# Three families of 512-column matrix products written as two 256-column products each, with new places for their weights

## The chip, the cores and the metric

The kernel runs on one core of one Trainium2 chip. The metric is device time in microseconds of a whole execution, as the median of several runs. A core has a matrix engine (TensorE; the profile shows its products as PE and its weight loads as PEld), VectorE (DVE), ScalarE (ACT), GpSimd (POOL) and queues of DMA transfers, of which SyncE's (SP) carries most here. Each engine works through its own list of instructions in order and waits at semaphores for the others.

## The reference

The kernel computes a two-layer encoder for one sequence of 512 tokens and 1024 channels, in float32. Cut to what matters:

```python
for l in range(DEPTH):                                   # 2 layers
    h = rmsnorm(x, attn_norm[l])
    sb_q, sb_k, sb_v, df_q, df_k, df_v = split(h @ w_in[l], 6)     # 512 columns each
    sb_out = stick_breaking_attention(sb_q, sb_k, sb_v)  # 8 heads of 64, sigmoid weights
    df_out = differential_attention(rope(df_q), rope(df_k), df_v, lam)  # 4 heads, two softmaxes
    df_out = rmsnorm(df_out, subln_norm[l]) * (1.0 - lambda_init)
    x = x + concat([sb_out, df_out]) @ w_o[l]            # output projection
    h = rmsnorm(x, mlp_norm[l])
    x = x + square(relu(h @ w_ff1[l])) @ w_ff2[l]        # 4096 hidden channels
return rmsnorm(x, final_norm)
```

## The kernel before, in words

**Split products.** Every float32 weight tile is split into a rounded high part and the low remainder (`whi` by ScalarE at L118, `wlo` by VectorE at L135), and so are the activations (`h_hi`, `h_lo` and others). A product of two float32 tiles is then three matmuls: high by high, high by low, low by high. The helper `three` (L303 to L312) issues them; lines 310, 311 and 312 are these three for nearly all products of the kernel, so the profile's groups tell them apart by the tile that they write. Each matmul has a weight load of its own for its stationary operand of 128 x 128; the moving operand has 256 or 512 columns.

**Walking.** `three` has a last argument `step`. If it is set, the output in PSUM and the moving operand are addressed in blocks of `step` columns from the last block to the first (`walked`). The result is the same.

**Weight units.** `_UNITS` lists every 128 x 1024 weight tile in order of use. The first letter says what it is: `x` differential query and key blocks, `p` stick-breaking query and key blocks, `v` stick-breaking values, `w` the values of the differential (softmax) heads, `o` the output projection, `1` and `s` the first dense layer (its first group whole, the others in quadrants, seven forms each), `f` the second dense layer. `split_part` takes a slot of 1024 + 64 columns for each part and cuts 1024 columns out of it. For the letters in `NARROW`, `s` and `v`, the high part begins at column 48 and the low part at column 16 (`PLACES`); for all others both begin at 0. So what the diff calls places are offsets of the split weights inside their slots, in float32 columns of 4 bytes.

**Which operand is which.** In the projections (`block`), the output projection (`wo`) and the first stage of the dense layer (`quad_group`), the weights are stationary and activations move. In both kinds of values (`values_of`, `all_values`) the activations are stationary and the weights move.

**Widths.** `quad_group` and `values_of` multiply 256 columns at a time, walked with a step of 32. `block`, `all_values` and `wo` multiply 512 columns at a time, not walked.

**Order of the work.** Two generators are merged by hand. `dense` yields after each chunk of projections, values and the output projection's first half (`wo(1)`), with an assumed time; `attn` yields score, transpose and value products. After each step of `dense` a credit decides how many steps of `attn` follow. So in the first 214 us of layer 0 (and the same stretch of layer 1), products of attention stand between the chunks. The output projection's second half, `wo(0)`, comes after attention with nothing in between. The assumed times are constants (0.216 us for a wide product) that the change leaves alone. Instructions written in this order are placed on the engines by a list scheduler; `behind` adds an ordering edge where the text wants one. The product that `all_values` keeps as `W.product` is such an anchor, for the transposes of the first norm.

Of the kernel before, what the change touches and what calls it, by code (L numbers as in the profile page):

```python
# [22 lines left out]
KC = D // P  # L23
# [13 lines left out]
MAN = ()  # L37
APART = (("s", 0, 1), ("s", 3, 0), ("s", 3, 1))
_CTX = {}
NARROW, PLACES, PAD = "sv", (48, 16), 64  # L40
DLY_R, DLY_D, DLY_S, DLY_Q = 3.5, 10.2, 9.0, 6.0
TAIL, ATT, DENSE, CAP = 6.0, 53.0, 145.0, 0.1
FORMS = ("11", "x3", "x2", "21", "x1", "x4", "22")
# [9 lines left out]
def _unit_list():  # L53
    units = []
    def qk(l, cq, ck, b):
        units.append(("p", l, cq + b * P))
        units.append(("p", l, ck + b * P))

    for l in range(L):
        for item in ORDER:  # L60
            b = int(item[1])
            if item[0] == "d":
                units.append(("x", l, b, 0))
                units.append(("x", l, b, 1))
            elif item[0] == "s":
                qk(l, SBQ, SBK, b)
            elif item[0] == "w":
                units.extend(("w", l, part) for part in range(4))
            else:
                units.extend(("v", l, SBV + b * P, half) for half in range(2))  # L70
        for half in (1, 0):
            for j in range(4):
                units.append(("o", l, half, j))
        for g in range(GROUPS):
            if g == 0:
                units.extend(("1", l, f) for f in range(2 * GP))
            else:
                units.extend(("s", l, g, j, form) for j in range(2) for form in FORMS)
            for form in FORMS2:
                for c in range(GP // 2):  # L80
                    units.append(("f", l, g, form, c))
    return units


_UNITS = _unit_list()
# [9 lines left out]
class _Weights:  # L95
# [24 lines left out]
    def split_part(self, i, a, b):  # L120
        nc = self.nc
        if i not in self.tiles and i in self.home:
            self.tiles[i] = self.home[i]
        if i not in self.tiles:
            k = self.spot(i)
            self.owner[k] = i
            self.turn = k + 1
            hi, lo = (
                self.pools[k // 2].tile([P, 1024 + PAD], F32R, tag=f"w{n}", name=f"w{n}{i}")[:, at : at + 1024]
                for n, at in zip(("hi", "lo"), PLACES if _UNITS[i][0] in NARROW else (0, 0)))  # L130
            self.tiles[i] = (hi, lo)
        hi, lo = self.tiles[i]
        raw = self.first if (i, b) == (0, P) else self.raw[i]
        h = self.round(hi[:, a:b], raw[:, a:b])
        self.last = h, nc.vector.tensor_tensor(  # L135
            out=lo[:, a:b], in0=raw[:, a:b], in1=hi[:, a:b].bitcast(F32), op=ALU.subtract)
# [31 lines left out]
def trunk(ctx, tc, opened, xT, w, w2, w1, gfin, lamv, cos, sin, out):  # L168
# [11 lines left out]
    def bank(tag, name):  # L180
        if tag == "any":
            tag = ("mm", "s", "s", "mm", "s")[turn[0] % 5]
            turn[0] += 1
        ring[0] += tag == "s"
        return ps.tile([P, 512], F32, tag=tag, name=name, bufs=banks[tag])
# [3 lines left out]
    W = _Weights(nc, w, wraw, wspl)  # L189
# [37 lines left out]
    def gcol(which, l, c):  # L227
        i = {"attn": l * 8, "mlp": 16 + l * 8, "final": 32, "sub": 40 + l}[which] + c
        return g_all[:, i : i + 1]
# [21 lines left out]
    def make_h(c, g):  # L251
        a = nc.scalar.activation(h_hi[:, c, :], x[:, c, :], AF.Copy, scale=g)
        return a, nc.vector.scalar_tensor_tensor(
            out=h_lo[:, c, :], in0=x[:, c, :], scalar=g, in1=h_hi[:, c, :].bitcast(F32),
            op0=ALU.mult, op1=ALU.subtract)

    def add_sq(c, first, sqt, eng=nc.gpsimd):
        if first:
            return nc.scalar.activation(ssq, x[:, c, :], AF.Square), None
        sq = sqt("sq")  # L260
        s = nc.scalar.activation(sq, x[:, c, :], AF.Square)
        return s, eng.tensor_tensor(out=ssq, in0=ssq, in1=sq, op=ALU.add)
# [35 lines left out]
    def walked(t, step):  # L298
        return t.rearrange("p (a b) -> p a b", b=step)[:, ::-1, :]
# [4 lines left out]
    def three(pt, a, b, first, last, goes_on=False, step=0):  # L304
        ah, al = a
        bh, bl = b
        if step:
            pt, bh, bl = (walked(e, step) for e in (pt, bh, bl))
        return (
            nc.tensor.matmul(pt, ah, bh, start=first, stop=False, skip_group_check=goes_on),  # L310
            nc.tensor.matmul(pt, ah, bl, start=False, stop=False, skip_group_check=goes_on),  # L311
            nc.tensor.matmul(pt, al, bh, start=False, stop=last, skip_group_check=goes_on))  # L312

    def hpair(c):
        return h_hi[:, c, :], h_lo[:, c, :]

    def wpair(u, c, n=P):
        return u[0][:, c * n : (c + 1) * n], u[1][:, c * n : (c + 1) * n]

    def block(name, tag="mm"):  # L320
        pt = bank(tag, name)
        u = W.next("px" if name[0] == "p" else "1")
        for c in range(KC):
            three(pt, wpair(u, c), hpair(c), c == 0, c == KC - 1)
            yield pt if c == KC - 1 else None

    def constants(a2):
# [18 lines left out]
    for l in range(L):  # L346
        with ExitStack() as actx:
# [49 lines left out]
            first = W.split  # L397
# [56 lines left out]
            def all_values():  # L454
                pts = [bank(tag, f"p{l}w{tb}") for tb, tag in enumerate(("s", "s", "s", "o"))]
                for part in range(4):
                    u = W.next("w")
                    for n in range(2):
                        c = 2 * part + n
                        wide = wpair(u, n, 512)  # L460
                        for tb, pt in enumerate(pts):
                            h = [e[:, c, tb * P : (tb + 1) * P] for e in (h_hi, h_lo)]
                            W.product = three(pt, h, wide, c == 0, c == KC - 1)[2]
                            if c == KC - 1:
                                hi, lo, r = vd_hi[:, tb, :], vd_lo[:, tb, :], rcol[:, tb : tb + 1]
                                nc.scalar.activation(hi, pt, AF.Copy, scale=r)
                                nc.vector.scalar_tensor_tensor(
                                    out=lo, in0=pt, scalar=r, in1=hi.bitcast(F32), op0=ALU.mult, op1=ALU.subtract)
                            yield
                for i in range(4):  # L470
                    ready[("vd", i)] = clock[0] + 2.5
# [323 lines left out]
            def wo(half):  # L795
                for j in range(4):
                    u = W.next("o")
                    for dd in range(2):
                        db = 2 * j + dd
                        pt = bank("mm" if half else "any", f"wo{l}{half}{db}")  # L800
                        for e in range(4):
                            a = u[0][:, e * 256 + dd * P : e * 256 + dd * P + P]
                            b_ = u[1][:, e * 256 + dd * P : e * 256 + dd * P + P]
                            mh, ml = (md_hi, md_lo) if half else (ms_hi, ms_lo)
                            three(pt, (a, b_), (mh[:, e, :], ml[:, e, :]), e == 0, e == 3)
                            if e < 3:
                                yield 3 * 0.216
                        nc.vector.tensor_add(x[:, db, :], x[:, db, :], pt)
                        if half == 0:
                            ends["h"] = make_h(db, gcol("mlp", l, db))  # L810
                            add_sq(db, db == 0, tt, nc.vector)
                        yield 3 * 0.216

            def dense(pts):
# [24 lines left out]
                for item in ORDER[1:]:  # L839
                    kind, b = item[0], int(item[1])  # L840
                    for which in ("qk" if kind in "ds" else "v"):
# [12 lines left out]
                        if kind in "ds":  # L854
                            {"s": evict_s, "d": evict_d}[kind](pt, kind, b, which)
                yield from wo(1)

            at = attn()
            done = 2 * KC * 3 * 0.216 if l else 0.0
            spent = credit = 0.0  # L860
            live = True
            for cost in dense(pts if l else None):
# [5 lines left out]
                while live and credit > 0:  # L868
                    c = next(at, None)
# [14 lines left out]
            for _ in wo(0):  # L884
                pass

        with ExitStack() as fctx:
# [3 lines left out]
            last = l == L - 1  # L891
# [327 lines left out]
            for g in range(GROUPS):  # L1219
# [24 lines left out]
                for form in FORMS2:  # L1244
# [20 lines left out]
                    for n, (c, i, r, part) in enumerate(work):  # L1265
                        if c not in held:
                            held[c] = W.next("f")
                        u = held[c]
                        hi, lo = (e[:, :, i, :] for e in sides[c])
                        rs = slice(r * P, r * P + P)  # L1270
                        mine = [m for m, e in enumerate(work) if e[2:] == (r, part)]
                        pt, b_ = to[r], wpair(u, i, 512)
                        if part:
                            pt = halves[part - 1][:, 0:256]
                            b_ = [e[:, 256 * part - 256 : 256 * part] for e in b_]
# [8 lines left out]
                        if end and not last and form == "22" and n % 2:  # L1284
                            h = back(n // 2)
# [19 lines left out]
                    if end and last and form == "x1":  # L1305
                        done = ((2, 0), (3, 0), (0, 1), (1, 1))
                        squares = [square(*e) for e in done]
                        weighed = [weigh(*e) for e in done]
                    elif end and last and form == "x4":
                        first = [came[0]]  # L1310
# [5 lines left out]
            else:  # L1316
# [6 lines left out]
                for n in range(KC):  # L1323
                    if n in (3, 5):
                        for c_ in (n + 1, n + 2):
                            h = back(c_)
# [81 lines left out]
```

## Time and profile before

| | |
|---|---|
| runs | median 1107.52 us of 3 (1106.96, 1107.52, 1112.36) |
| profiled execution | 1108.1 us, its span 1106.3 us |
| granted TensorE clock | 0.999 of full speed |
| TensorE products | 6345, busy 1098.0 us |
| TensorE weight loads | 6345, busy 959.4 us |
| VectorE, ScalarE, GpSimd | busy 906.8, 688.1, 151.9 us |

The span is from the first to the last instruction of the program. A product's row in the timeline has its start and its modelled duration; since products are pipelined, the duration is longer than the distance to the next start. In a name such as `wo<-mdh,whi` the output comes first, then the two operands. `p0s1q` is layer 0's stick-breaking query block 1, `p0u` layer 0's stick-breaking values, `p0w` its softmax values, `wo` the output projection, `X`, `V` and `Y` the banks of the dense layers.

### The profile page before, as it was taken

Reading aid. Unit: us, or ns where it says so; the run is one execution under the profiler, and the core shown is the slowest. Engines: PE = TensorE matmul, PEld = TensorE weight load, DVE = VectorE, ACT = ScalarE, POOL = GpSimd, SP = SyncE. Lnnn points to the kernel's source line nnn. Section 1 sums busy time; section 2 is a strip of 40 time slices with the busy share of each in tenths; the row PEclk is TensorE's granted clock in tenths of the full one; section 3 lists DMA queues with packets and bytes.
Section 4 is the critical chain, followed back from the end, with each engine's and each line's share of the span. In section 5 each row is a group of like instructions: output and inputs, shape, how many; then the busy total and the mean of one; then the engine's idle time right before and its main releaser. Section 6 shows DMA issues by size and latency. Waiting matters only on the chain.

```text
span 1106.3 us, 17170 instructions
## 1 busy us (share of the span) xinstructions
PE 1098.0 (99%) x6345; PEld 959.4 (87%) x6345; DVE 906.8 (82%) x1333; ACT 688.1 (62%) x1131; POOL 151.9 (14%) x233
## 2 busy tenths in 40 slices
PE   9999999999999999999999999999999999999997
PEld 7889889888899899899778898888888998998986
DVE  7799688798669879779877897887797798797797
ACT  6447777567658458467345576675674584574775
POOL 1001343101011001001000013530010110010010
PEclk9999999999999999999999999999999999999999
DMA  7466343269777788758325654522577787787462
GB/s 248 144 191 190 113 127 107 84 213 230 183 212 186 182 209 185 196 138 212 113 76 142 190 164 123 164 77 77 197 176 180 211 183 186 202 188 196 130 133 96
DMA packets 61044, 181.25 MB, mean 164 GB/s; under 512 B 7456, under 2 KB 8736, under 8 KB 60960
## 3 DMA queue, kind: packets, MB, share of 16 engines
q1 hardware_dynamic: 50160, 141.84, 41.1%
q0 software_dynamic: 10368, 37.75, 19.7%
q8 instruction: 50, 0.82, 0.3%
q10 hardware_dynamic: 432, 0.56, 0.1%
q14 instruction: 34, 0.28, 0.1%
HBM read 150.77 MB, written 4.19 MB: 140 GB/s over the span
## 4 chain that ended last, share of the span: by engine, by line
PE 93%; issue 3%; DVE 2%; DMA 2%; ACT 0%; POOL 0%; POOLq 0%; DVEq 0%; ACTq 0%
PE X L310 8%; PE X L311 8%; PE X L312 8%; PE V L311 3%; PE V L312 3%; PE V L310 3%; PE wo L310 3%; PE wo L311 3%; PE wo L312 3%; PE f L312 3%; PE f L310 3%; PE f L311 3%; PE Y L312 2%; PE Y L311 2%; PE Y L310 2%
## 5 line engine op out<-in xcount | busy, mean ns | idle before, releaser
L118 ACT ACTIVATE whi<-q 128x1024 fp32r<-128x1024 f32 x96 | 101.3, 1056 | 101.7 <-PE X L312 39.3
L135 DVE TENSOR_TENSOR wlo<-q,whi 128x1024 fp32r<-128x1024 f32 x96 | 116.8, 1221 | 43.0 <-ACT whi L118 42.8
L135 DVE TENSOR_TENSOR wlo<-raw,whi 128x1024 fp32r<-128x1024 f32 (+1 forms) x82 | 96.7, 1185 | 6.7 <-ACT whi L118 6.4
L118 ACT ACTIVATE whi<-raw 128x1024 fp32r<-128x1024 f32 (+1 forms) x82 | 80.8, 994 | 33.6 <-issue 17.9
L310 PE MATMUL X<-whi,Ah 128*128 128x512 f32 x248 | 97.6, 393 | 0.0
L312 PE MATMUL X<-whi,Al 128*128 128x512 f32 x248 | 96.7, 390 | 0.0
L311 PE MATMUL X<-wlo,Ah 128*128 128x512 f32 x248 | 96.6, 390 | 0.0
L135 DVE TENSOR_TENSOR wlo<-waves,whi 128x1024 fp32r<-128x1024 f32 x40 | 48.8, 1221 | 15.4 <-ACT whi L118 15.3
L118 ACT ACTIVATE whi<-waves 128x1024 fp32r<-128x1024 f32 x40 | 42.2, 1056 | 29.2 <-PE X L312 18.9
L310 PEld LDWEIGHTS X<-whi,Ah 128*128 128x128 f32 x248 | 46.5, 188 | 12.1 <-DVE y L1132 1.9
L312 PEld LDWEIGHTS X<-whi,Al 128*128 128x128 f32 x248 | 46.6, 188 | 9.9
L311 PEld LDWEIGHTS X<-wlo,Ah 128*128 128x128 f32 x248 | 46.6, 188 | 8.9
L311 PE MATMUL X<-h_lo,whi 128*128 128x256 f32 x192 | 53.0, 276 | 0.0
L310 PE MATMUL X<-h_hi,whi 128*128 128x256 f32 x192 | 53.0, 276 | 0.0
L312 PE MATMUL X<-hxh,wlo 128*128 128x256 f32 x192 | 53.0, 276 | 0.0
L310 PE MATMUL X<-hxh,whi 128*128 128x256 f32 x192 | 53.0, 276 | 0.0
L312 PE MATMUL X<-h_hi,wlo 128*128 128x256 f32 x192 | 53.0, 276 | 0.0
L311 PE MATMUL X<-hxl,whi 128*128 128x256 f32 x192 | 53.0, 276 | 0.0
L310 PE MATMUL f<-h_hi,whi 128*128 128x512 f32 x128 | 50.4, 394 | 0.0
L312 PE MATMUL f<-h_hi,wlo 128*128 128x512 f32 x128 | 49.9, 390 | 0.0
L311 PE MATMUL f<-h_lo,whi 128*128 128x512 f32 x128 | 49.8, 389 | 0.0
L242 DVE TENSOR_TENSOR Al<-x,Ah 128x512 fp32r<-128x512 f32 (+1 forms) x60 | 46.5, 792 | 3.7 <-ACT Ah L241 3.5
(764 smaller groups left out, 3686.7 us busy)
## 6 DMA issues: line engine op xcount, KB each, us to landing
raw<-in_w SPq DMA_DIRECT2D x78, 512.0 KB, 3.6
q<-in_w SPq DMA_DIRECT2D x48, 512.0 KB, 4.5
q<-in_w POOLq DMA_DIRECT2D x48, 512.0 KB, 8.5
waves<-in_w SPq DMA_DIRECT2D x28, 512.0 KB, 4.6
first_a<-in_w SPq DMA_DIRECT2D x12, 512.0 KB, 4.8
first_b<-in_w SPq DMA_DIRECT2D x12, 512.0 KB, 5.4
first_c<-in_w SPq DMA_DIRECT2D x12, 512.0 KB, 4.4
first_b<-in_w POOLq DMA_DIRECT2D x12, 512.0 KB, 6.7
```

Source lines behind the costliest of these rows:

```text
L118: return self.nc.scalar.activation(o, src, AF.Copy)
L135: self.last = h, nc.vector.tensor_tensor(out=lo[:, a:b], in0=raw[:, a:b], in1=hi[:, a:b].bitcast(F32), op=ALU.subtract)
L242: nc.vector.tensor_tensor(out=lo, in0=src, in1=hi.bitcast(F32), op=ALU.subtract)
L310: nc.tensor.matmul(pt, ah, bh, start=first, stop=False, skip_group_check=goes_on),
L311: nc.tensor.matmul(pt, ah, bl, start=False, stop=False, skip_group_check=goes_on),
L312: nc.tensor.matmul(pt, al, bh, start=False, stop=last, skip_group_check=goes_on))
```

## The change

`PLACES` becomes a table by letter. `p` and `o` get the pair (48, 16) that `s` has; `w` gets (16, 48); `v` goes from (48, 16) to (16, 48). A new helper `three_halves` issues the three products for the columns 0 to 255 and then for 256 to 511, each walked with a step of 32; only the very first opens the bank and only the very last closes it. The stick-breaking query and key blocks, the softmax values and the output projection call it in place of `three`. The differential blocks (`x`) and the dense layers keep what they had.

```diff
-NARROW, PLACES, PAD = "sv", (48, 16), 64
+PLACES, PAD = {"s": (48, 16), "p": (48, 16), "o": (48, 16), "v": (16, 48), "w": (16, 48)}, 64
...
-                for n, at in zip(("hi", "lo"), PLACES if _UNITS[i][0] in NARROW else (0, 0)))
+                for n, at in zip(("hi", "lo"), PLACES.get(_UNITS[i][0], (0, 0))))
...
+    def three_halves(pt, a, b, first, last):
+        for n in range(2):
+            cols = slice(256 * n, 256 * n + 256)
+            done = three(pt[:, cols], a, [e[:, cols] for e in b], first and n == 0, last and n == 1, True, 32)
+        return done
...
+        some = three_halves if _UNITS[W.used][0] == "p" else three
         u = W.next("px" if name[0] == "p" else "1")
         for c in range(KC):
-            three(pt, wpair(u, c), hpair(c), c == 0, c == KC - 1)
+            some(pt, wpair(u, c), hpair(c), c == 0, c == KC - 1)
...
-                            W.product = three(pt, h, wide, c == 0, c == KC - 1)[2]
+                            W.product = three_halves(pt, h, wide, c == 0, c == KC - 1)[2]
...
-                            three(pt, (a, b_), (mh[:, e, :], ml[:, e, :]), e == 0, e == 3)
+                            three_halves(pt, (a, b_), (mh[:, e, :], ml[:, e, :]), e == 0, e == 3)
```

## The prediction

> **What bounds the kernel now.** I read the page's head, its busy times and its chain of waits first, then the groups of TensorE instructions by line and shape, then the starts in the timeline of the stages that the change touches.
>
> ```profile
> span 1106.3 us, 17170 instructions
> PE 1098.0 (99%) x6345; PEld 959.4 (87%) x6345; DVE 906.8 (82%) x1333; ACT 688.1 (62%) x1131; POOL 151.9 (14%) x233
> PE 93%; issue 3%; DVE 2%; DMA 2%; ACT 0%; POOL 0%; POOLq 0%; DVEq 0%; ACTq 0%
> ```
>
> TensorE streams matmuls through the whole span, and 93% of the chain that ended last is its own. So the price of this change is the distance between the starts of successive products (I call it the pitch), times their number. Busy microseconds and mean durations overlap, because one product starts before the last one's modelled end; the pitch has to be read from starts.
>
> The pitch of a 512-column product where nothing is mixed in, from the output projection's second half in layer 0:
>
> ```profile
> 214.75 0.39 PE L310 MATMUL wo<-vdh,whi 128*128 128x512 f32 x1
> ...
> 236.51 0.39 PE L310 MATMUL f<-h_hi,whi 128*128 128x512 f32 x1
> L310 PE MATMUL wo<-vdh,whi x32: 389/389/389, 214.7 to 235.8; 128*128 128x512 f32 x32
> ```
>
> Three lines of 32 products each lie between those starts: (236.51 - 214.75) / 96 = 226.7 ns, and each lasts 389 ns. The pitch of a 256-column product in the walked form and at the first stage's places, which is the form the change copies:
>
> ```profile
> 318.79 0.28 PE L310 MATMUL X<-h_hi,whi 128*128 128x256 f32 x1
> 318.90 0.28 PE L311 MATMUL X<-h_lo,whi 128*128 128x256 f32 x1
> 319.02 0.28 PE L312 MATMUL X<-h_hi,wlo 128*128 128x256 f32 x1
> 319.14 0.28 PE L310 MATMUL X<-h_hi,whi 128*128 128x256 f32 x1
> ...
> 356.88 0.39 PE L310 MATMUL X<-whi,Ah 128*128 128x512 f32 x1
> ```
>
> Two quad groups of 168 products lie between 318.79 and 356.88 (7 forms, 2 pairs, 4 chunks, 3 products each): 38.09 / 336 = 113.4 ns. Two of them make 226.7 ns, the same as one wide product to 0.1 ns. The first two after the switch from wide products are slower (0.11 and 0.12), and from the third start on the pitch is constant: this form falls into step in two products.
>
> Two other rows show that 113.4 ns belongs to this form and these places and is not what 256 columns cost anywhere:
>
> ```profile
> 97.17 0.28 PE L312 MATMUL p0u<-whi,h_lo 128*128 128x256 f32 x1
> ...
> 99.05 0.28 PE L562 MATMUL S0d<-st0d3k,st0d3q 128*128 128x256 f32 x1
> 1097.50 0.28 PE L312 MATMUL Z<-whi,Al 128*128 128x256 f32 x1
> ...
> 1098.70 0.28 PE L310 MATMUL half<-whi,Ah 128*128 128x256 f32 x1
> ```
>
> The stick-breaking values (walked too, but with the weights as moving operand at 48 and 16) take 1.88 us for 16 starts, 117.5 ns. The last, unwalked 256-column pieces take 1.20 us for 10 starts, 120 ns.
>
> **The change, part by part.** Three families of 512-column products become pairs of halves: the stick-breaking query and key blocks (16 blocks of 8 chunks of 3 = 384), the softmax values (2 layers, 4 parts, 2 chunks, 4 banks, 3 = 192) and the output projection (2 layers, 2 halves, 8 columns, 4 chunks, 3 = 384). That is 960 matmuls and 960 weight loads more. The values of the stick-breaking heads (384 halves) keep their number and swap their pair of places.
>
> *What hides nothing and what costs nothing.* No DMA, wait, PSUM bank or eviction is added; a bank is still released by the last product of its group, which starts 113 ns later and lasts 276 ns instead of 389, so it ends when it did. The splits write at other offsets; their time does not depend on it:
>
> ```profile
> L118 ACT ACTIVATE whi<-raw x82: 295/1060/1107, 4.9 to 812.8; 128x1024 fp32r<-128x1024 f32 x74, 128x256 fp32r<-128x256 f32 x7, 128x128 fp32r<-128x128 f32 x1
> L118 ACT ACTIVATE whi<-first_a x24: 1060/1062/1064, 310.8 to 1040.0; 128x1024 fp32r<-128x1024 f32 x24
> ```
>
> The raw ones go to place 0 (all but the few value units), the first-stage ones to place 48, with medians of 1060 and 1062 ns. The added weight loads are one a half already in the rows at 113.4, so their cost is inside that figure.
>
> *Quiet stretches.* Half of the output projection (192 products) runs undisturbed at 226.7, and so do nearly all the softmax values, whose rows stand at the same 389 to 390 ns:
>
> ```profile
> L311 PE MATMUL p0w<-wlo,h_hi 128*128 128x512 f32 x16 | 6.2, 390 | 0.0
> L310 PE MATMUL p0w<-mdh,h_hi 128*128 128x512 f32 x16 | 5.9, 389 | 0.0
> ```
>
>  Projections and output projection have weights stationary and 256 contiguous activation columns moving, as the first stage has, and all these tiles are allocated on multiples of 256 bytes, so the distance between the address loaded and the address streamed is the first stage's. The values have the roles reversed, and the pair (16, 48) reversed with them, which makes the same distances, modulo 256 bytes, for high and low parts (64 bytes one way for the high, the other way for the low). So I price these halves at 113.4: 384 products x (2 x 113.4 - 226.7) = 0.0 us.
>
> *Stretches mixed with attention.* There the wide products are above their floor:
>
> ```profile
> L310 PE MATMUL p0s1q<-h_hi,whi 128*128 128x512 f32 x8 | 3.2, 404 | 0.0
> L312 PE MATMUL p0s1q<-h_hi,wlo 128*128 128x512 f32 x8 | 3.2, 394 | 0.0
> L311 PE MATMUL p0s1q<-h_lo,whi 128*128 128x512 f32 x8 | 3.2, 394 | 0.0
> L310 PE MATMUL wo<-mdh,whi 128*128 128x512 f32 x64 | 26.4, 412 | 0.0
> L312 PE MATMUL wo<-mdh,wlo 128*128 128x512 f32 x64 | 25.2, 394 | 0.0
> L311 PE MATMUL wo<-mdl,whi 128*128 128x512 f32 x64 | 25.2, 394 | 0.0
> L310 PE MATMUL p0u<-whi,h_hi 128*128 128x256 f32 x64 | 18.3, 286 | 0.0
> ```
>
> A mean above 389 ns (276 for halves) is pitch lost. For one projection block: 8 x (15 + 5 + 5) = 0.2 us, 3.2 us over 16 blocks; for the first half of the output projection: 64 x (23 + 5 + 5) = 2.1 us. A part of it is no loss: a product behind a row of transposes starts late only because the last transpose took too little.
>
> ```profile
> 137.34 0.93 PE L661 MATMUL T0s<-edge,sig0s 128*128 128x128 f32 x7
> 138.10 0.60 PE L273 MATMUL rs_d<-edge,sqo 128*128 128x128 f32 x4
> 138.46 0.48 PE L310 MATMUL p0s2k<-h_hi,whi 128*128 128x512 f32 x1
> 138.78 0.39 PE L311 MATMUL p0s2k<-h_lo,whi 128*128 128x512 f32 x1
> ```
>
> Eleven transposes end their starts in 1.12 us, and the next product then holds 0.32 us. Taking that 0.09 us off the 20 projections and 14 output products that stand so leaves about 1.5 us of true loss in the projections and 1.0 in the output projection. In the stick-breaking values it is 384 x (117.5 - 113.4) = 1.6 us.
>
> The halves would lose their first two pitches after every attention step, as at 318.79: together some 11 ns more than 226.7. The projections stand in 84 unbroken runs, the output projection in 55 mixed ones, and the stick-breaking values in 50, counted over the starts from the first to the last of these rows:
>
> ```profile
> 77.93 0.39 PE L310 MATMUL p0s0q<-h_hi,whi 128*128 128x512 f32 x1
> ...
> 710.71 0.39 PE L312 MATMUL p1s3k<-h_hi,wlo 128*128 128x512 f32 x1
> ```
>
> So: projections -1.5 + 84 x 0.011 = -0.6 us; output projection -1.0 + 55 x 0.011 = -0.4; stick-breaking values, whose new pair gives them the first stage's distance, -1.6 + 50 x 0.011 = -1.0. **Sum -2.0 us.** The unknown is the pitch of new halves in mixed stretches, bounded below by 113.4 with no falling into step to pay (-4.1 us in all) and above by the 117.5 of the stick-breaking values as they are now. I take the value near the lower end, because the cause that separates 113.4 from 117.5 in these rows, as far as the code shows, is the distance of addresses, and the change sets it to the first stage's everywhere.
>
> The profiled execution took 1108.1 us, 1.8 outside its 1106.3 us span, and the median of the runs is 1107.5. With 2.0 off: a span near 1104.3, a profiled execution near 1106.1 and a median of **1105.5 us**.
>
> **Rivals.**
>
> *Halves do not fall into step between attention steps.* Then they stand near the 117.5 ns of the stick-breaking values, which never settle although they come in runs of 6 to 18. For it: those values are the largest family of halves that the trace shows in this company. Against it: they have the other distance. Price, against the true mean of wide ones (389 + 3.9 and 389 + 5.2 ns in duration, so 230.6 and 231.9 in pitch): 384 x (235 - 230.6) + 192 x (235 - 231.9) = +2.3 us, and the swapped values gain nothing. It decides from 115.5 ns a half on. Time: 1109.8. If the quiet 384 products stayed out of step as well, 384 x 8.3 ns = 3.2 us more: 1113.0.
>
> *All halves are at the floor at once.* The whole 4.1 us go, and what the neighbouring score and value products lose to phase goes with it, bounded by another microsecond from their small number. For it: no engine other than TensorE is near its limit. Against it: the first two halves at 318.79. Time: 1102.4.
>
> *Every product pays a fixed price, whatever its form.* The nearest rows are the unwalked pieces at 120 ns: a pair of them takes 240, 13.3 ns more than a wide product, and 960 such pairs cost 12.8 us; the mixed stretches give back at most their 2.5. Time: 1117.8. For it: those pieces come from the same kind of product as the wide ones beside them. Against it: the 336 walked halves at 113.4, whose pair shows a price of 0.1 ns. The Trainium skill, page "TensorE: Matmul & The Clock Gate", section "Back-to-back issue gap", states such a price: a warm pitch of N / 2.4 + 2.5 ns, by which a pair costs 2.5 ns more than one product of 512, an estimate of 2.4 us over the 960 (1109.9). The trace does not agree with it: the formula gives 215.8 and 109.2 ns where the rows show 226.7 and 113.4.
>
> *The order of other engines moves.* The program's instructions are placed by a list scheduler that estimates durations; more, shorter products could change what VectorE and ScalarE do first. The longest wait of TensorE for a split shows what one such shift can cost:
>
> ```profile
> PEld V L311 <- DVE wlo L135: 1.2, 1, 1.2
> ```
>
> With TensorE at 99% busy such waits are rare; I give this case 1.2 us either way, 1108.7 at the upper end without the gain.
>
> **How the numbers follow.** The forecast 0.58; halves out of step 0.20 (a quarter of it in the quiet stretches as well); all at the floor 0.10; a fixed price 0.04; order 0.08. The range goes from the floor case to the first form of the slower one, with 0.4 us below and 1.2 above for pitches that were read from few rows: 1102.0 to 1111.0. It leaves out the two dear cases, 0.09. A difference of 0.5%, 5.5 us, is about what a measurement can tell from no change; the bounds are 1102.0 and 1113.1. Faster than that takes the floor case and something more, 0.06; slower takes halves out of step everywhere or the fixed price, 0.06; within, 0.88.
>
> **What would show each step right or wrong.** Matmuls should number 7305. Right: the output projection's second half still runs from 214.75 to about 236.5 in length (21.8 us), now in 192 starts at 113.4; the rows of the stick-breaking values drop from means of 280 to 286 ns to about 277; the halves of projections have means near 278. Wrong: means of 280 and more in the projections (out of step), a pitch of 115 or more in the quiet output projection (a fixed price or another distance), or new waits of TensorE on ScalarE's or VectorE's splits. What would make the prediction wrong as a whole is a pitch that follows something other than those distances: then the swapped values would not move, and the new halves could stand anywhere between 113 and 120 ns.

## The result, and the profile after

The changed kernel takes 1113.13 us (median of 6 runs, 1112.8 to 1113.53) against 1107.41 us for the kernel before beside it (median of 6, 1106.96 to 1112.36): a ratio of 1.005, with a 95% interval of 1.0039 to 1.0060. It is 5.7 us slower. The forecast was 1105.5 us in a range of 1102.0 to 1111.0, so the direction was wrong and the time lies outside the range. The profiled execution of the kernel before was one of its slower ones (1108.1 us, 0.7 above this median), so differences between the two traces come out somewhat smaller than 5.7 us.

The head of the changed kernel's profile, its busy times and its chain of waits by engine:

```profile
span 1111.4 us, 19077 instructions
PE 1102.3 (99%) x7305; PEld 1004.2 (90%) x7305; DVE 906.9 (82%) x1333; ACT 687.6 (62%) x1131; POOL 153.8 (14%) x233
PE 88%; DVE 5%; ACT 2%; DMA 2%; POOL 2%; issue 1%; SPq 0%; DVEq 0%; POOLq 0%; ACTq 0%
```

There are 7305 products, as announced, and the other engines do the same work in nearly the same time. The span grew by 5.1 us. In the chain TensorE's share fell from 93% to 88%, and VectorE's rose from 2% to 5%: the chain now passes through VectorE more often. That is the first sign of new waits.

The groups of the new halves (last columns: busy us, mean ns of one, idle us just before). A half that starts 113.4 ns after the last one reads 276 ns:

```profile
L310 PE MATMUL p0w<-whi,h_hi 128*128 128x256 f32 x32 | 9.0, 282 | 0.0
L311 PE MATMUL p0w<-wlo,h_hi 128*128 128x256 f32 x32 | 9.0, 282 | 0.0
L311 PE MATMUL p0w<-mdl,h_hi 128*128 128x256 f32 x32 | 8.9, 283 | 0.0
L310 PE MATMUL p0u<-whi,h_hi 128*128 128x256 f32 x64 | 18.4, 287 | 0.0
L310 PE MATMUL wo<-vdh,whi 128*128 128x256 f32 x128 | 35.3, 276 | 0.0
L311 PE MATMUL wo<-mdl,whi 128*128 128x256 f32 x128 | 35.8, 279 | 0.0
L310 PE MATMUL p0s1q<-h_hi,whi 128*128 128x256 f32 x16 | 4.5, 283 | 0.0
L311 PE MATMUL p0s1q<-h_lo,whi 128*128 128x256 f32 x16 | 4.5, 278 | 0.0
```

Only the output projection's quiet half (`vdh`) is at 276. The softmax values (`p0w`) stand at 282, though nothing is mixed into them, and the stick-breaking values (`p0u`) stand where they stood (287, before 286). The timeline gives the pitches:

```profile
29.98 0.28 PE L310 MATMUL p0w<-whi,h_hi 128*128 128x256 f32 x1
...
33.16 0.28 PE L310 MATMUL p0w<-whi,h_hi 128*128 128x256 f32 x1
...
218.35 0.28 PE L310 MATMUL wo<-vdh,whi 128*128 128x256 f32 x1
...
240.12 0.39 PE L310 MATMUL f<-h_hi,whi 128*128 128x512 f32 x1
...
1104.58 0.28 PE L312 MATMUL half<-whi,Al 128*128 128x256 f32 x1
```

Between the first two rows lie 27 halves of the softmax values: 3.18 / 27 = 117.8 ns. Between the next two lie the 192 halves of the quiet output projection: 21.77 / 192 = 113.4 ns, as forecast. The last row is the last product; before it started at 1100.02, so 4.56 us of the loss lie ahead of it, and the other 0.5 us of span behind it.

The rows of waits (engine, tile and line, what it waited for: us in total, times, longest) that the changed kernel has and the kernel before has not, or has smaller:

```profile
PEld rb_d L295 <- POOL rc L282: 0.8, 2, 0.4
PEld T0s L668 <- DVE turned L242: 0.4, 1, 0.4
PEld T1s L668 <- DVE turned L242: 0.4, 1, 0.4
PEld p1w L311 <- DVE mdl L135: 0.4, 1, 0.4
PEld O0s L699 <- DVE mt L715: 0.3, 1, 0.3
```

The 1.2 us wait of `V` for `wlo` that the prediction showed is gone. One of the new waits reads like this in the timeline:

```profile
155.50 0.68 DVE L715 TENSOR_TENSOR mt<-O0s,oc 64x512 f32<-64x512 f32 x1 [0.46 <-ACT hl0s2q L241]
...
155.89 0.28 PE L312 MATMUL p0s3q<-h_hi,wlo 128*128 128x256 f32 x1
156.24 0.39 PE L699 MATMUL O0s<-turned,vs 128*128 128x256 f32 x1
```

The value product at 156.24 waits for `mt`, and `mt` started only after ScalarE had written `hl0s2q`, work for other heads. TensorE's starts stand 0.35 us apart instead of 0.11.

**Where the 4.56 us came from.** For every product I took the distance to the next start and subtracted its floor (226.7 ns for 512 columns, half of that for 256, 109 for a transpose). What is left over is called a wait above 45 ns, and phase below. One execution of each kernel, in us:

| part | before | after | difference |
|---|---|---|---|
| softmax values, phase | 0.2 | 1.9 | +1.8 |
| stick-breaking values, phase | 1.65 | 1.8 | +0.2 |
| output projection, phase | 1.0 | 1.3 | +0.3 |
| stick-breaking projections, phase | 1.55 | 1.75 | +0.2 |
| everything else, phase | 4.05 | 3.4 | -0.65 |
| waits of attention's products and of the projections beside them | 0.7 | 3.8 | +3.1 |
| wait of `V` for `wlo` | 1.1 | 0.0 | -1.1 |
| other waits (opening, softmax values, dense layers) | 4.4 | 5.2 | +0.8 |

Most of the +0.8 of other waits is the opening's and says nothing of the change. The first softmax value starts at 16.99 us here and at 16.51 before, but it starts just as late, at 16.98, in a kernel that differs from the one before in two places of weights alone, and in no instruction's order (the fourth experiment). Where the -0.65 of phase in everything else comes from was not followed.

So there are two causes: halves that do not reach the pitch they were given (+1.8 in the softmax values, and +1.8 of phase in all), and waits that were not there (+3.1 around attention and the projections, less the 1.1 at `V` that went away). The lag can be followed at the same product in both traces: first stick-breaking projection +1.7, last one of layer 0 +3.6, unchanged through layer 0's dense layer (+3.6), +2.5 at the last norm's transposes of that layer (the wait of `V` is no longer needed, as TensorE arrives later than its data), end of layer 1's softmax values +3.4, last projection of layer 1 +4.4, last product +4.6. The dense layers, where nothing was changed, neither add nor give back, but for that one wait.

### The profile page after: what moved, and what is told of

Read it like the earlier page. It is cut to its first block, busy times and chain, and to the rows that moved or that the text cites. A ratio compares the mean times of both kernels' runs of the same rounds, so it can differ in the third digit from the quotient of the medians.

```text
span 1111.4 us, 19077 instructions
## 1 busy us (share of the span) xinstructions
PE 1102.3 (99%) x7305; PEld 1004.2 (90%) x7305; DVE 906.9 (82%) x1333; ACT 687.6 (62%) x1131; POOL 153.8 (14%) x233
## 4 chain that ended last, share of the span: by engine, by line
PE 88%; DVE 5%; ACT 2%; DMA 2%; POOL 2%; issue 1%; SPq 0%; DVEq 0%; POOLq 0%; ACTq 0%
PE X L310 9%; PE X L312 9%; PE X L311 9%; PE V L310 3%; PE V L311 3%; PE V L312 3%; PE wo L312 3%; PE wo L310 3%; PE wo L311 3%; PE f L312 3%; PE f L310 3%; PE f L311 3%; PE Y L312 2%; PE Y L311 2%; PE Y L310 2%
```

## Experiments

### One part at a time

Four kernels make one part of the change each; everything else is as before.

Only the softmax values as halves:

```diff
+PLACES, PAD = {"s": (48, 16), "v": (48, 16), "w": (16, 48)}, 64
...
-                            W.product = three(pt, h, wide, c == 0, c == KC - 1)[2]
+                            W.product = three_halves(pt, h, wide, c == 0, c == KC - 1)[2]
```

> Only the softmax values are halved, at their new places; projections, output projection and stick-breaking values are as before. Theory A (halves whose weights move never settle): means of 280 to 282 ns in the value rows instead of 276, about +1.8 us of pitch, so 1.5 to 2.5 us slower than before. Theory B (the loss is waits behind a new order of the other engines' instructions): only 9 instructions of VectorE and 1 of ScalarE stand elsewhere here, so nothing beyond the pitch. Theory C (each added product costs the same, 5.7 us / 960 = 5.9 ns): 192 x 5.9 ns = +1.1 us.

Measured: 1109.52 us beside 1107.38, ratio 1.0017 (1.0007 to 1.0026), 0.8 to 2.9 us slower. Their group in the profile of this kernel:

```profile
L311 PE MATMUL p0w<-wlo,h_hi 128*128 128x256 f32 x32 | 9.0, 282 | 0.0
```

The mean is that of the full change. The step "softmax values 0.0" is wrong by itself, without the rest.

Only the stick-breaking projections as halves:

```diff
+PLACES, PAD = {"s": (48, 16), "v": (48, 16), "p": (48, 16)}, 64
...
+        some = three_halves if _UNITS[W.used][0] == "p" else three
```

> Only the stick-breaking projections are halved, at their new places. Theory A: pitch within 0.3 us of before. Theory B: 44 instructions of VectorE and 12 of ScalarE stand elsewhere, so the new waits of score, value and transpose products (about 2 us in the changed kernel) are here: +1.5 to +2.5 us. Theory C: 384 x 5.9 ns = +2.3 us spread evenly over the projections' own rows, without waits.

Measured: 1111.11 beside 1107.38, ratio 1.0030 (1.0021 to 1.0040), 2.3 to 4.4 us slower. This is the largest part. The rows of waits of this kernel:

```profile
PEld rb_d L295 <- POOL rc L282: 0.7, 2, 0.4
PEld T0s L668 <- DVE turned L242: 0.4, 1, 0.4
PEld T1s L668 <- DVE turned L242: 0.4, 1, 0.4
```

Three of the five new waits of the full change are here already (the one for `turned` in layer 0 was 0.2 in the kernel before).

Only the output projection as halves, and only the swap of the stick-breaking values' places:

```diff
+PLACES, PAD = {"s": (48, 16), "v": (48, 16), "o": (48, 16)}, 64
...
-                            three(pt, (a, b_), (mh[:, e, :], ml[:, e, :]), e == 0, e == 3)
+                            three_halves(pt, (a, b_), (mh[:, e, :], ml[:, e, :]), e == 0, e == 3)
```

> Only the output projection is halved, at its new places. Theory A: its quiet half unchanged, its half mixed with attention +0.3 us. Theory B: 12 instructions of VectorE and 8 of ScalarE stand elsewhere, so little more: 0 to +0.7 us. Theory C: 384 x 5.9 ns = +2.3 us.

```diff
+PLACES, PAD = {"s": (48, 16), "v": (16, 48)}, 64
```

> Only the places of the stick-breaking values are swapped; the order of all engines is that of before. Theory A: the swap moves nothing, means stay at 279 to 286 ns, time within 0.3 us of before. The theory of the prediction (the distance of addresses sets the pitch): means of 277 ns, 1.0 us faster. Theory C: no product is added, no difference.

Measured: 1107.94 beside 1107.38, ratio 1.0005 (0.9996 to 1.0014), and 1107.98, ratio 1.0003 (0.9994 to 1.0013). Neither can be told from no change. The swap did not move its group by more than 1 ns:

```profile
L310 PE MATMUL p0u<-whi,h_hi 128*128 128x256 f32 x64 | 18.4, 287 | 0.0
L311 PE MATMUL p0u<-wlo,h_hi 128*128 128x256 f32 x64 | 18.0, 281 | 0.0
```

The -1.0 us forecast for it is not there. The four ratios add up to 1.0055 against 1.0050 for the whole; within the intervals, the parts act side by side.

### Is it the order of the other engines?

In the compiled programs the same instructions stand at another place in their engine's list: with only the projections changed, 12 of ScalarE, 44 of VectorE and 6 of SyncE; with the whole change 21, 65 and 8; with only the swap none. (With only the output projection changed, 8 of ScalarE and 12 of VectorE moved, and that cost nothing that can be measured: not every move costs.) To see what that costs, the kernels were built with ordering edges that chain an engine's instructions in the order of the kernel before (`PIN` lists that order):

```diff
+def pin(tc, nc):
...
+    for name, runs in PIN.items():
+        order = [made[name][a + n] for a, many in runs for n in range(many)]
...
+        for b, a in zip(order, order[1:]):
+            tc.add_manual_dep(a, b.name, mybir.DependencyInfo(
+                mybir.DependencyClass.NoSync, mybir.DependencyReason.DATA), reason="order")
...
+        pin(tc, nc)
```

First for ScalarE, VectorE and SyncE alone, on the whole change and on the projections alone:

> The changed kernel, with ordering edges that give ScalarE, VectorE and SyncE exactly the order of instructions that they have in the kernel before. Theory B (the rest of the loss is waits that follow from the new order): the waits of transposes, scores and values fall back by about 2 us, the pitch of the softmax values stays, so 1109.5 to 1111.0. Its rival (the order is harmless, and it is the shorter products that bring TensorE to those points before the other engines are ready): 1113 as the changed kernel, with the same waits.

> Only the stick-breaking projections are halved (the part that cost 3.7 us alone), with the same edges, so that the other engines keep the order of the kernel before. Theory B: the loss of 3.7 us goes but for 0.2 us of pitch and the score step that TensorE itself takes elsewhere: 1107.5 to 1108.5. Its rival: 1111, unchanged.

Measured: the whole change 1112.35 beside 1107.80, ratio 1.0038 (1.0023 to 1.0053); the projections alone 1109.14, ratio 1.0014 (1.0004 to 1.0023). The projections gave back about half of their loss. Both times lie above what was expected: a remainder was left, and TensorE's own list also differed, in a few places where score products, the first stick-breaking value products and transposes stand. So the same again with TensorE's list chained too, two halves in each wide product's place:

> Only the stick-breaking projections are halved, and now TensorE too keeps the order of the kernel before, each wide product's place being taken by two halves. Theory B (the loss of this part is the order of instructions): what is left of it, 1.3 us with only the other engines in order, goes: within 0.5 us of before. Its rival (something in the halves themselves makes later products wait): still about 1.3 us slower, with waits of transposes and scores of 1.5 us.

> The changed kernel with all engines in the order of the kernel before. Theory A with B: what stays is pitch, 1.8 us in the softmax values and some 0.6 in the rest: 1109.8 to 1110.5. The rival of B: 1112 and more.

Measured: the projections alone 1107.53 beside 1107.29, ratio 1.0000 (0.9991 to 1.0010); the whole change 1110.75, ratio 1.0034 (1.0023 to 1.0046). The waits of the projections kernel in this order:

```profile
PEld V L311 <- DVE wlo L135: 1.4, 2, 1.0
PEld T0s L668 <- DVE turned L242: 0.2, 1, 0.2
```

The wait for `rc` is gone, the one for `turned` is halved, and the 1 us wait of `V` is back, as in the kernel before. For the projections this settles it: their 2.3 to 4.4 us were the order of instructions, and the halves themselves cost and gain nothing that can be measured, which here means nothing beyond about 1 us either way. For the whole change the order accounts for about 2 us (5.7 less 3.5), but the two intervals overlap, so this size is not firm. What stays is the softmax values' pitch and one longer wait:

```profile
PEld p1w L311 <- DVE mdl L135: 1.1, 1, 1.1
```

This wait belongs to the softmax values, not to the order: it stands in the traces of all kernels that halve them (0.3 to 0.4 us in the first experiment, the whole change and its first ordered form) and in none that leaves them wide. Why it is 1.1 us in this order was not followed. Here the last product starts 2.3 us later than before: +1.8 from the softmax values' phase, -0.3 from all other phase, +0.8 from waits.

### What sets the pitch of a half?

The prediction took the distance between the address loaded and the address streamed as the cause. Four kernels vary what it held equal. Their times are single runs, and only the pitches are used. All but the last leave the softmax values wide.

*The walk.* Projections and output projection as halves at the new places, but not walked:

```diff
-            done = three(pt[:, cols], a, [e[:, cols] for e in b], first and n == 0, last and n == 1, True, 32)
+            done = three(pt[:, cols], a, [e[:, cols] for e in b], first and n == 0, last and n == 1, True, 0)
```

> Projections and output projection are halved at their new places but not walked; both kinds of values as before. If walking makes the difference: 120 ns a half (means of 283) in the quiet output projection, 384 x 6.6 = 2.5 us there and as much in the other products, so about 1114 to 1116. If the places alone do it: 113.4.

Measured: 1113.07 us. The quiet output projection of layer 0 and that of layer 1, each with 192 halves between its two rows:

```profile
217.46 0.28 PE L310 MATMUL wo<-vdh,whi 128*128 128x256 f32 x1
...
239.22 0.40 PE L310 MATMUL f<-h_hi,whi 128*128 128x512 f32 x1
...
766.25 0.28 PE L310 MATMUL wo<-vdh,whi 128*128 128x256 f32 x1
...
789.07 0.40 PE L310 MATMUL f<-h_hi,whi 128*128 128x512 f32 x1
```

Layer 0: 21.76 / 192 = 113.3 ns. Layer 1: 22.82 / 192 = 118.9 ns. The code, the sizes and the places (modulo 256 bytes) are the same in both, each pitch holds from the first half to the last, and the last halves of the mixed stretch ahead already ran at it. So there are two pitches that keep themselves up, and a stretch keeps the one that it has when it begins; what made the two layers differ is not shown. Walked, in the changed kernel, both layers run at 113.4.

*The place.* Projections and output projection walked, with their weights at place 0, and the stick-breaking values at (0, 0):

```diff
+PLACES, PAD = {"s": (48, 16), "v": (0, 0)}, 64
```

> Projections and output projection are halved and walked, with their weights at place 0; the softmax values as before, the stick-breaking values at place 0. If the offset of the weights makes the difference: 118 to 120 ns a half in the quiet output projection. If walking alone does it: 113.4. In the stick-breaking values, with moving weights on a multiple of 256 bytes but no distance to the stationary operand: 118 to 120 as at the other two pairs.

Measured: 1114.73 us. The same 192 halves in layer 0:

```profile
217.56 0.28 PE L310 MATMUL wo<-vdh,whi 128*128 128x256 f32 x1
...
240.34 0.39 PE L310 MATMUL f<-h_hi,whi 128*128 128x512 f32 x1
```

22.78 / 192 = 118.6 ns, and 118.7 in layer 1. The walk alone is not enough; the place is needed. Projections and stick-breaking values stand at 118.7 too, the latter 1.2 ns above their 117.5 before.

*Is it a matter of 256 columns?* The projections and the output projection walked and at the new places, but still with 512 columns:

```diff
+    def walked_wide(pt, a, b, first, last):
+        return three(pt, a, b, first, last, False, 32)
```

> Projections and output projection stay 512 columns wide, but are walked in blocks of 32 with their weights at the first stage's places; both kinds of values as before. All engines keep the order of the kernel before. If walking takes the 6.6 ns off a wide product that it takes off a narrow one (120 to 113.4): 220 ns of pitch in the quiet output projection and 5 us faster over 768 products. If 226.7 is a floor of 512 columns: no difference, or slower by the blocks.

Measured: 1108.81 us beside 1107.80. The 96 wide products of layer 0's quiet output projection:

```profile
214.71 0.39 PE L310 MATMUL wo<-vdh,whi 128*128 128x512 f32 x1
...
236.97 0.39 PE L310 MATMUL f<-h_hi,whi 128*128 128x512 f32 x1
```

22.26 / 96 = 231.9 ns, where the unwalked ones at place 0 take 226.7. Walk and places together do not help wide products; they cost them 2%. It is not told apart here which of the two does.

*The start of the moving operand.* In the values the roles are reversed: activations are loaded, weights move. Their weights begin 64 or 192 bytes past a multiple of 256, their activations on one. This kernel moves the offset to the other operand: the activations `h` begin at 192 (high) and 64 bytes (low), the values' weights at 0, those of the projections and of the first dense stage at 128 bytes (attention has one buffer less for its sigmoids and probabilities, for room). The distances stay: for the softmax values, and for the first stage where `h` moves, two of every three products in turn have 64 bytes one way and the third has 64 the other way, as in the changed kernel:

```diff
+PLACES, PAD = {"s": (32, 32), "p": (32, 32), "o": (48, 16)}, 64
...
+    cp.tile([P, 16], F32, tag="gap0", name="gap0")
...
+    cp.tile([P, 32], F32, tag="gap1", name="gap1")
...
+    cp.tile([P, 48], F32, tag="gap2", name="gap2")
```

> The changed kernel with the high activations moved to 192 and the low ones to 64 bytes past a multiple of 256, the weights of both kinds of values at place 0 and those of first stage and projections at 32, and one buffer less of attention's probabilities. For both kinds of values the moving operand then starts on a multiple of 256 bytes and the stationary one at the distances that the weights have in the first stage: the first stage's case with the roles exchanged. If distance and start of the moving operand set the pitch: means of 276 to 277 ns in those rows. If a pitch of 113.4 needs something else of the first stage: 280 to 282 as before. In the first stage and the projections the distance is kept and the moving start changes: 276 if distance alone counts.

Measured: 1125.35 beside 1107.80. Softmax values in the timeline, then the groups of the stick-breaking values and of the first stage:

```profile
29.45 0.28 PE L312 MATMUL p0w<-whi,h_hi 128*128 128x256 f32 x1
...
32.86 0.28 PE L312 MATMUL p0w<-whi,h_hi 128*128 128x256 f32 x1
```

```profile
L313 PE MATMUL p0u<-wlo,h_hi 128*128 128x256 f32 x64 | 17.8, 279 | 0.0
L312 PE MATMUL X<-h_hi,whi 128*128 128x256 f32 x192 | 53.9, 280 | 0.0
L313 PE MATMUL X<-h_lo,whi 128*128 128x256 f32 x192 | 54.2, 282 | 0.0
L312 PE MATMUL X<-hxh,whi 128*128 128x256 f32 x192 | 54.4, 283 | 0.0
```

The softmax values now run at 3.41 / 30 = 113.7 ns, the parts in tiles of their own included (277 to 280 ns in their groups in layer 0), and the stick-breaking values fall to 115.6 over all and 114.3 from the seventh half of a run on (117.5 and 117.6 before). In exchange the first stage rises from 113.4 to 118.7, over its 2016 halves in two layers 10.8 us (6.3 of them in the 1152 halves of bank `X`). In the rows with `h_hi` and `h_lo` the distances are as before, but now the moving operand starts 192 or 64 bytes past a multiple of 256 and the loaded one 128, and they left 276 ns for 280 and 282. So the distance alone is not what decides. What the fast stretches share is that the moving operand starts on a multiple of 256 bytes (walked, that is its lowest address) and the loaded one 64 or 192 bytes past one. This is what the traces have in common and not a mechanism that was shown.

The experiments did not lead to a version that beats both kernels. Of the parts changed here, the stick-breaking values have the most left to gain (1.65 us of phase in the whole kernel, 0.15%); in the last experiment they did, at the price of the first stage, since both read the same `h`. A second copy of `h` for one of them was not tried.

## Why the prediction was wrong

It was wrong in two of its steps, and each of them was one sentence.

**"So I price these halves at 113.4" for the softmax values, by the same distance modulo 256 bytes: 0.0 us forecast, +1.8 measured.** Two things failed. The distance alone does not set the pitch, as the shifted activations show: same distance, 113.7 with the offset on the loaded operand, 117.8 with it on the moving one. And the first of the two pairs of parts (`mdh`, `mdl`) lies in tiles of its own that `split_part` does not pad, so the new places never reach it; it ran at 281 to 284 ns in layer 0, like the rest. The stick-breaking values as they were before already stood against the step: weights moving, off by 64 and 192 bytes, 117.5 ns. The prediction read that row as "the other distance", where "the other role" explained it as well.

**"No DMA, wait, PSUM bank or eviction is added", and a moved order priced at 1.2 us with a chance of 0.08.** The order did move, on TensorE, VectorE, ScalarE and SyncE, and in the projections alone it cost 2.3 to 4.4 us. The mechanism was on record as a rival; what failed was its price and its chance. The price was the longest single wait of TensorE for a split. Once dozens of instructions have moved, the cost is a sum of small ones: in the 3.1 us of new waits around attention no row of the profile is above 0.8.

The other steps:

- *Quiet output projection, 0.0*: right, 113.4 in both layers. Unwalked it would have been right in layer 0 alone.
- *Projections, -0.6*: with the order held, the run time is the same as before and the phase +0.2. The term mis-sized is falling into step, put at 11 ns a run. Measured, the first six halves after a break take 115.6, 118.6, 115.7, 114.5, 115.2 and 117.2 ns, 17 ns above six at the floor, and a run has 8 to 9 halves on average. Three wide products lose about 15 after the same break, so nothing is left to gain.
- *Output projection, -0.4*: +0.3 of phase, of the same kind; in its mixed half the pitch is 116.6 ns, waits left out.
- *Stick-breaking values, -1.0*: +0.2; the pitch went from 117.5 to 118.0. This rested on the distance as well.
- *A fixed price per product*: falls, with the 192 quiet halves at 113.4 and the projections in their old order at a ratio of 1.0000.
- *Halves out of step everywhere*, 1113.0: the time is hit almost exactly, by accident. It was right that the softmax values do not fall into step; but it had the quiet output projection out of step too, which it is not, and no waits.

The prediction itself named what would overturn it: a pitch that follows something else than the distances, "then the swapped values would not move". They did not.

## What to carry to other kernels

A tile that runs fast was copied here with its offsets, and the offsets were worth nothing where the operands' roles were reversed (117.8 ns in place of 113.4); before a layout is copied, look in the trace for a family that has the same roles, and if there is none, let the range reach to the slow pitch. Where a scheduler places instructions, an edit of one engine's products is an edit of all engines' lists: compare the lists of the two compiled programs, and measure once with the old order held, before anything is said of the edit itself. With an engine 99% busy, a change of sub-microsecond terms has no cushion, and a sum of waits of a few tenths of a microsecond decides.

## What the runs showed of the hardware that was not expected

The pitch of a 256-column product, with a weight load of its own each, by what was varied (quiet output projection unless said; mean ns from start to start; the bytes of a pair are those of the high and low part, and of a walked operand those of its lowest address):

| walked | loaded operand, bytes past a multiple of 256 | moving operand | pitch |
|---|---|---|---|
| yes | 192 and 64 | 0 | 113.4 |
| no | 192 and 64 | 0 | 113.3 in layer 0, 118.9 in layer 1 |
| yes | 0 | 0 | 118.6 |
| no | 0 | 0 | 120 (the last pieces, before) |
| yes | 0 | 64 and 192 (softmax values) | 117.8 |
| yes | 192 and 64 | 0 (softmax values, shifted `h`) | 113.7 |
| yes | 128 | 192 and 64 (first stage, shifted `h`) | 116.3 to 119.7 by form |
| yes | 128 | 0 (first stage, the forms that move `hx`) | 119.2 to 120.0 |

Two pitches, 113.4 and about 119, both hold for hundreds of products. The walk does not decide how fast a stretch can be, since one unwalked stretch ran at 113.3. At the places 192 and 64 all ten walked quiet stretches in five traces ran at 113.4, and one of two unwalked ones did, so the walk seems to decide whether a stretch gets there; two unwalked stretches are few. Which storage or port makes the difference is not shown.

The Trainium skill, page "TensorE: Matmul & The Clock Gate", section "Step-by-step: what each phase is for", says that loading the next weights takes no read bandwidth from the running product. By that alone one would not expect the place of the loaded weights to matter; here the same 192 products run at 113.4 or 118.6 ns, and within them nothing differs but that place. Whether it is bandwidth that they share, no run here shows.
